# The second product of each filter tap contracts 128 rows instead of 64

## The chip, the cores and the metric

The kernel runs on one core of a Trainium2 chip. The metric is the time of one execution on the device in microseconds; a comparison uses the median of several runs. The engines of the core are named as in the profile: PE is TensorE (matrix products), PEld its weight loads, DVE is VectorE, ACT is ScalarE, POOL is GpSimd, and SP issues most of the DMA transfers.

## The reference, cut to what matters

The whole program is one layer: an input projection of 2048 tokens, a long convolution (branch A), a chunked gating unit (branch B) and an output projection. The change lies in the filter of the long convolution. Three sine layers give 64 features for each of 2048 positions, and one more product gives the taps of 1024 channels in both directions, which then decay with the position:

```python
def hyena_filter(L, w1, b1, fr1, w2, b2, fr2, w3, b3, fr3, w_o):
    ...
    h = jnp.sin(fr3.astype(f32) * (h @ w3.astype(f32) + b3.astype(f32)))
    h = h @ w_o.astype(f32)
    ...
    h_fwd = h[:, :D_A] * decay
    h_bwd = h[:, D_A:] * decay
    l1 = jnp.sum(jnp.abs(h_fwd), axis=0) + jnp.sum(jnp.abs(h_bwd[1:]), axis=0)
    k = jnp.concatenate([h_fwd, jnp.zeros((1, D_A), f32), h_bwd[1:][::-1]], axis=0)
    return k / (l1[None, :] + EPS)
```

## The kernel before

Tokens are kept as 16 groups j of 128. Every operand of a large product is split into a high part `hi` and a low part `lo` in the type float32r, and a product is three passes: hi by hi, lo by hi, hi by lo (`mm3`, L157 to L159).

The foreground is the input projection: 56 blocks of weights, each in four chunks of 512 tokens, each chunk 8 times `mm3` into one bank of PSUM. One chunk is a step. In the background run staged jobs, generators that are moved on by one stage at each step. The order in which the instructions of an engine stand is then settled by a scheduler that mixes foreground and background; on the chip each engine takes them in that fixed order.

The filter taps are the background of the first part (`k1_jobs`, with the foreground `ug_phase`). The channels go in two halves of 512. `k1_weights` loads the 64 rows of the filter's last weights twice, into rows 0 to 63 and again into rows 64 to 127 of `wr`, for each of the two directions d, and splits it into `hi` (ACT) and `lo` (DVE). Then 16 jobs `k1_job`, one for each j, two directions in each, so 2 x 16 x 2 = 64 taps products:

- `gd` (128 rows: the 64 features' high part in rows 0 to 63, their low part in rows 64 to 127) comes from DRAM by a DMA on POOL's queue (L444), in two buffers; `dd`, the decay, by a DMA on SP's queue (L446), also in two buffers.
- L452 multiplies all 128 rows of `gd` by all 128 rows of `wh`, which gives high by high and low by high in one product. L453 adds high by low: rows 0 to 63 of `gd` by rows 0 to 63 of `wl`. In the profile the rows of L452 read `a<-hi,gd` and those of L453 `a<-lo,gd`.
- DVE multiplies by the decay (L454), adds and subtracts the directions (L456, L457), ACT and DVE split the results (L150, L152), ACT takes the absolute value (L460) and DVE adds it to the running L1 sum (L461), which is the last reader of `dd`.
- A stage later the first step of a Fourier transform follows on PE: two `mm3` (rows `b<-hi,f` and `b<-lo,f`), copied out by ACT (L482) and written to DRAM (L483).

The job for j = 0 comes last in each half; it also takes the sum over all positions by two plain float32 products (L468).

Of the kernel before, what the change touches and what calls it, by code (L numbers as in the profile page):

```python
"""Hyena / gMLP hybrid block on one NeuronCore.  # L1

Tokens are kept in the order (j, p) with t = 16 p + j.  Every large product runs
as three float32r passes over operands split exactly into a high and a low part.
The long convolution is a 4096-point real DFT done as 256 x 16: one step over p,
one over j, a product of spectra, and the two steps back.
"""
# [5 lines left out]
F32 = mybir.dt.float32  # L13
# [17 lines left out]

# ---------------------------------------------------------------- constants
def _split(a):
# [76 lines left out]

# ------------------------------------------------------------------- kernel
class Body:
    """Foreground: the input projection, one chunk of 512 tokens a step.
    Background: staged jobs, each moved on by one stage a step."""

# [7 lines left out]

    # -- scheduling of the trace
    def go(self, job):
# [19 lines left out]

    # -- small helpers
    def split(self, eng, raw, pool, tag, bufs, copy=None):
        """Two float32r tiles whose sum is raw."""
        hi = pool.tile(list(raw.shape), F32R, name="hi", tag=tag, bufs=bufs)
        (copy or self.nc.scalar.copy)(hi, raw)  # L150
        lo = pool.tile(list(raw.shape), F32R, name="lo", tag=tag, bufs=bufs)
        eng.tensor_tensor(lo, raw, hi.bitcast(F32), op=ALU.subtract)  # L152
        return hi, lo
# [18 lines left out]

    # -- whole program
    def build(self):
# [82 lines left out]

    # -- x: RMS norm, transposed, split
    def x_phase(self, xs):
# [46 lines left out]

    # -- input projection
    def prep_w(self, blk, pool=None, tag="w", bufs=5, copy=None):
# [5 lines left out]
    def project(self, blk, nxt):  # L314
        """Yields (n, psum) of the block's four chunks of 512 tokens."""
        b, wh, wl = self.wq.pop(0)
        assert b == blk
        for n in range(4):
            if n == 1 and nxt is not None:
                self.prep_w(nxt)  # L320
            ps = self.bank("proj")
            for k in range(8):
                self.mm3(ps, wh[:, k], wl[:, k], self.xh[n][:, k], self.xl[n][:, k], k == 0, k == 7)
            yield n, ps

    # -- branch B: u * silu(gate)
    def ug_first(self, fg, xs):
# [5 lines left out]
    def silu(self, pool, ps, tag="sg", bufs=5):  # L333
        s = pool.tile([128, 512], F32, name="sg", tag=tag, bufs=bufs)
        self.nc.scalar.activation(s, ps, AF.Silu)
        return s
# [14 lines left out]

    # -- Hyena filter: features through the sine MLP
    def mlp(self, mp):
# [61 lines left out]

    # -- filter taps with decay, L1 norm, first DFT step
    def k1_jobs(self, kp):
# [10 lines left out]
    def k1_weights(self, kp, cs, st):  # L428
        nc, i = self.nc, self.i
        wo = i["filt_w_out"].rearrange("q (d c) -> q d c", d=2)[:, :, cs]  # L430
        st["w"] = []
        for d in range(2):
            wr = kp.tile([128, 512], F32, name="wr", tag="kq", bufs=10)
            for r in range(2):
                nc.sync.dma_start(wr[64 * r:64 * r + 64], wo[:, d])
            st["w"].append(self.split(nc.vector, wr, kp, "kw", 4))
        st["l1"] = kp.tile([128, 2, 512], F32, name="l1")
        nc.gpsimd.memset(st["l1"], 0.0)
        yield

    def k1_job(self, kp, cs, st, j):
        nc = self.nc
        gd = kp.tile([128, 2, 128], F32R, name="gd", bufs=2)
        nc.gpsimd.dma_start(gd, self.GD[j])  # L444
        dd = kp.tile([128, 2, 512], F32, name="dd", bufs=2)
        nc.sync.dma_start(dd, self.i["c_dec"][j][:, :, cs])  # L446
        yield
        l1 = st["l1"]
        for d in range(2):
            wh, wl = st["w"][d]  # L450
            ps = self.bank("a")
            nc.tensor.matmul(ps, gd[:, d], wh, start=True, stop=False)  # L452
            nc.tensor.matmul(ps, gd[0:64, d], wl[0:64], start=False, stop=True)  # L453
            nc.vector.tensor_tensor(dd[:, d], ps, dd[:, d], op=ALU.mult)  # L454
        s = [kp.tile([128, 512], F32, name="s", tag="kq", bufs=10) for _ in range(2)]
        nc.vector.tensor_tensor(s[0], dd[:, 0], dd[:, 1], op=ALU.add)  # L456
        nc.vector.tensor_tensor(s[1], dd[:, 0], dd[:, 1], op=ALU.subtract)  # L457
        if j:
            parts = [self.split(nc.vector, x, kp, "kq", 10) for x in s]
        nc.scalar.activation(dd, dd, AF.Abs)  # L460
        nc.vector.tensor_tensor(l1, l1, dd, op=ALU.add)  # L461
        if j == 0:
            sk = kp.tile([1, 512], F32, name="sk", tag="kq", bufs=10)
            nc.sync.dma_start(sk, self.i["hyena_skip"][cs].rearrange("(o c) -> o c", o=1))
            yield
            ps = self.bank("a")
            for d in range(2):
                nc.tensor.matmul(ps, self.ones, l1[:, d], start=d == 0, stop=d == 1)  # L468
            le, ri = l1[0:1, 0], l1[0:1, 1]
            nc.vector.tensor_scalar(le, ps[0:1], EPS, None, op0=ALU.add)  # L470
            nc.vector.tensor_tensor(sk, sk, le, op=ALU.mult)
            nc.vector.reciprocal(ri, le)
            nc.sync.dma_start(self.RB[cs].rearrange("(o c) -> o c", o=1), ri)
            for d in range(2):
                nc.vector.tensor_tensor(s[d][0:1], s[d][0:1], sk, op=ALU.add)
            parts = [self.split(nc.vector, x, kp, "kq", 10) for x in s]
        yield
        for d in range(2):
            ps = self.bank("b")
            self.mm3(ps, self.f1[:, 0, d], self.f1[:, 1, d], *parts[d])  # L480
            ev = kp.tile([128, 512], F32, name="ev", tag="kq", bufs=10)
            nc.scalar.copy(ev, ps)  # L482
            nc.sync.dma_start(self.AK[128 * d:128 * d + 128, j, cs], ev)  # L483

    # -- short convolution over a raw block with halo
    def halo(self, raw):
# [25 lines left out]
    def staggered(self, jobs):  # L512
        """One job a step."""
        for job in jobs:
            self.go(job)
            yield

    # -- branch A: u = conv(x1) conv(v), first DFT step
    def xv_phase(self):
# [37 lines left out]

    # -- branch A: conv(x0) * silu(gate) / l1
    def xg_phase(self):
# [18 lines left out]

    # -- branch B: layer norm, position mixing, gate
    def vb_phase(self):  # L580
# [33 lines left out]
    def gated(self, h, n, vr, ug):  # L614
        """Tokens 4 n .. of head h: the mixed values times u silu(gate)."""
        uv = ug.rearrange("d (j b p) -> d j b p", j=4, b=16)
        self.nc.vector.tensor_tensor(uv, uv, vr[:, :, 4 * n:4 * n + 4].rearrange("d b j p -> d j b p"), op=ALU.mult)
        self.nc.sync.dma_start(self.Y[4 * n:4 * n + 4, :, 8 + h].rearrange("j d p -> d j p"), ug.rearrange("d (j p) -> d j p", j=4))
# [40 lines left out]

    # -- second DFT step of both, product of spectra, first step back  # L660
    def fft_jobs(self, hf):
# [39 lines left out]

    # -- last DFT step, gate
    def inv_jobs(self):
# [30 lines left out]

    # -- output projection, post norm, residual
    def load_wo(self, n):
        """Rows 512 n .. of w_out, where chunk n of x was."""
        nc = self.nc
        hi = self.xp.tile([128, 4, D], F32R, name=f"woh{n}", tag=f"xh{n}")
        lo = self.xp.tile([128, 4, D], F32R, name=f"wol{n}", tag=f"xl{n}")  # L740
# [8 lines left out]
    def out_mms(self, ps, h, r, hi, lo):  # L749
        """Channel blocks 4 r .. of the products for half h of the outputs."""  # L750
        sl = slice(h * 512, h * 512 + 512)
        for q in range(4):
            self.mm3(ps, hi[:, q], lo[:, q], self.xh[r][:, q, sl], self.xl[r][:, q, sl], r == 0 and q == 0, r == 3 and q == 3)

    def first_tokens(self, j, rs):
        """Channel blocks 4 r .. of tokens j, split."""
        if j not in self.yq:
# [20 lines left out]
    def out_phase(self, op):  # L778
# [9 lines left out]
        ld = lambda: op.tile([128, 8, 128], F32, name="yraw", bufs=4)  # L788
        # What is wanted first lies where memory is free first.
        first = {"z": [z()], 0: [xt(0)], 3: [q(3)], 1: [xt(1)], 2: [q(2)], "ld": [ld()]}  # L790
# [74 lines left out]
```

## Time and profile before

| | |
|---|---|
| runs shown | 2061.54 us median of 3 (2061.28 to 2063.18) |
| span of the profiled execution, first to last instruction | 2056.8 us |
| median less span | 4.7 us |
| PE busy | 2011.0 us, 98% of the span |
| DVE, ACT, POOL busy | 1158.9, 765.2, 228.3 us |
| granted TensorE clock, mean | 0.997 |
| taps products on L452 and L453 | 64 each, between 139 and 449 us |

The page gives no time of its own for the profiled execution beside its span; the runs' times also hold what lies ahead of the first and behind the last instruction. Matrix products are pipelined, and a product's duration includes its way through the array, so what counts on PE is the distance from one start to the next.

### The profile page before, as it was taken

Reading aid. Unit: us, or ns where it says so; the run is one execution under the profiler, and the core shown is the slowest. Engines: PE = TensorE matmul, PEld = TensorE weight load, DVE = VectorE, ACT = ScalarE, POOL = GpSimd, SP = SyncE. Lnnn points to the kernel's source line nnn. Section 1 sums busy time; section 2 is a strip of 40 time slices with the busy share of each in tenths; the row PEclk is TensorE's granted clock in tenths of the full one; section 3 lists DMA queues with packets and bytes.
Section 4 is the critical chain, followed back from the end, with each engine's and each line's share of the span. In section 5 each row is a group of like instructions: output and inputs, shape, how many; then the busy total and the mean of one; then the engine's idle time right before and its main releaser. Section 6 shows DMA issues by size and latency. Waiting matters only on the chain. (4 is left out here: it accounts for less than half of the span.)

```text
span 2056.8 us, 24610 instructions
## 1 busy us (share of the span) xinstructions
PE 2011.0 (98%) x9000; PEld 1612.7 (78%) x9000; DVE 1158.9 (56%) x1906; ACT 765.2 (37%) x1333; POOL 228.3 (11%) x223
## 2 busy tenths in 40 slices
PE   6999999999999999999999999999999999999998
PEld 5776777778888877877777778878888887888887
DVE  7357555553333477788777766555666664322221
ACT  7134334333333455555444444343222243111111
POOL 1011011011000111111111111101101000101000
PEclk9999999999999999999999999999999999999999
DMA  6155434441222355445544544543546454522311
GB/s 212 48 146 193 145 118 148 144 141 57 62 62 62 108 154 152 144 145 171 160 150 149 152 156 154 164 149 118 164 144 202 149 169 165 185 83 92 113 62 41
DMA packets 189705, 274.22 MB, mean 133 GB/s; under 512 B 18027, under 2 KB 93803, under 8 KB 189551
## 3 DMA queue, kind: packets, MB, share of 16 engines
q1 hardware_dynamic: 175184, 250.56, 37.5%
q0 software_dynamic: 14112, 21.50, 4.3%
q8 instruction: 71, 1.16, 0.2%
q10 hardware_dynamic: 288, 0.59, 0.1%
q14 instruction: 50, 0.41, 0.1%
HBM read 179.26 MB, written 93.33 MB: 133 GB/s over the span
## 5 line engine op out<-in xcount | busy, mean ns | idle before, releaser
L157 PE MATMUL proj<-xh,hi 128*128 128x512 f32 x1792 | 710.4, 396 | 0.0
L158 PE MATMUL proj<-xh,lo 128*128 128x512 f32 x1792 | 703.0, 392 | 0.0
L159 PE MATMUL proj<-xl,hi 128*128 128x512 f32 x1792 | 702.5, 392 | 0.0
L157 PEld LDWEIGHTS proj<-xh,hi 128*128 128x128 f32 x1792 | 337.2, 188 | 74.1 <-issue 8.3
L159 PEld LDWEIGHTS proj<-xl,hi 128*128 128x128 f32 x1792 | 336.8, 188 | 70.4 <-issue 1.0
L158 PEld LDWEIGHTS proj<-xh,lo 128*128 128x128 f32 x1792 | 337.2, 188 | 68.9 <-issue 2.8
L152 POOL TENSOR_TENSOR lo<-wraw,hi 128x1024 fp32r<-128x1024 f32 x56 | 135.7, 2423 | 599.9 <-ACT hi L150 599.7
L158 PE MATMUL proj<-woh,q 128*128 128x512 f32 x448 | 174.4, 389 | 0.0
L159 PE MATMUL proj<-wol,q 128*128 128x512 f32 x448 | 174.3, 389 | 0.0
L157 PE MATMUL proj<-woh,q 128*128 128x512 f32 x448 | 174.1, 389 | 0.0
L152 DVE TENSOR_TENSOR lo<-raw,hi 128x512 fp32r<-128x512 f32 x192 | 133.3, 720 | 43.2 <-ACT hi L150 43.1
L499 DVE SCALAR_TENSOR_TENSOR t<-raw,cw,t 128x512 f32<-128x512 f32 x96 | 80.3, 840 | 108.1 <-ACT raw L490 54.4
L150 ACT CAST hi<-raw 128x512 fp32r<-128x512 f32 x192 | 112.1, 622 | 27.9 <-DMA raw<-BY 23.1
L507 ACT COPY raw<-proj 128x512 f32<-128x512 f32 x96 | 56.2, 587 | 166.4 <-PE proj L159 158.8
L150 ACT CAST hi<-pa 128x512 fp32r<-128x512 f32 x64 | 39.8, 622 | 200.0 <-DVE pa L693 187.3
L150 ACT CAST hi<-wraw 128x1024 fp32r<-128x1024 f32 x55 | 57.9, 1054 | 136.7 <-PE proj L158 84.1
L689 DVE TENSOR_TENSOR pa<-u,b 64x512 f32<-64x512 f32 x128 | 87.6, 684 | 37.0 <-PE b L159 18.7
L158 PEld LDWEIGHTS proj<-woh,q 128*128 128x128 f32 x448 | 84.1, 188 | 17.8 <-DVE q L801 0.3
L159 PEld LDWEIGHTS proj<-wol,q 128*128 128x128 f32 x448 | 84.1, 188 | 17.5
L157 PEld LDWEIGHTS proj<-woh,q 128*128 128x128 f32 x448 | 84.1, 188 | 17.3
L689 DVE TENSOR_TENSOR pb<-u,b 64x512 f32<-64x512 f32 x128 | 87.9, 686 | 1.9
L157 PE MATMUL b<-hi,tv 128*128 128x512 f32 x192 | 80.8, 421 | 8.0 <-ACT hi L150 6.4
(160 smaller groups left out, 2518.8 us busy)
## 6 DMA issues: line engine op xcount, KB each, us to landing
wraw<-in_w_in_dram SPq DMA_DIRECT2D x56, 512.0 KB, 3.7
xt<-in_x_dram SPq DMA_DIRECT2D x32, 512.0 KB, 4.9
dd<-in_c_dec_dram SPq DMA_DIRECT2D x32, 512.0 KB, 4.0
AK<-ev SPq DMA_DIRECT2D x64, 256.0 KB, 3.1
tv<-in_c_tv_dram POOLq DMA_DIRECT2D x64, 256.0 KB, 4.3
AU<-ev SPq DMA_DIRECT2D x64, 256.0 KB, 2.8
raw<-AU SPq DMA_DIRECT2D x64, 256.0 KB, 4.2
raw<-AK SPq DMA_DIRECT2D x64, 256.0 KB, 3.3
```

What stands on the lines that cost most here:

```text
L150: (copy or self.nc.scalar.copy)(hi, raw)
L152: eng.tensor_tensor(lo, raw, hi.bitcast(F32), op=ALU.subtract)
L157: t.matmul(ps, sh, mh, start=first, stop=False)
L158: t.matmul(ps, sl, mh, start=False, stop=False)
L159: t.matmul(ps, sh, ml, start=False, stop=last)
L499: nc.vector.scalar_tensor_tensor(v, raw[:, j0:j0 + 4], wv(0), v, op0=ALU.mult, op1=ALU.add)
L507: self.nc.scalar.copy(raw[:, 1 + 4 * n:5 + 4 * n].rearrange("q j p -> q (j p)"), ps)
L689: nc.vector.tensor_tensor(o, uu, kk, op=ALU.mult)
```

## The change

The low part of the weights, `lo`, gets zeros in rows 64 to 127 (a MEMSET on POOL of 64 x 512 for each of the two directions in each of the two halves, four in all, L437 of the changed kernel), and the second product takes all 128 rows of both operands. The added rows multiply the low part of the features by zero, so the sum stays what it was. Nothing else is edited but comments; behind the edit the lines of the changed kernel are two higher (L452 becomes L454, L453 becomes L455).

```diff
@@ k1_weights
             for r in range(2):
                 nc.sync.dma_start(wr[64 * r:64 * r + 64], wo[:, d])
-            st["w"].append(self.split(nc.vector, wr, kp, "kw", 4))
+            hi, lo = self.split(nc.vector, wr, kp, "kw", 4)
+            nc.gpsimd.memset(lo[64:128].bitcast(F32), 0.0)
+            st["w"].append((hi, lo))
@@ k1_job
             nc.tensor.matmul(ps, gd[:, d], wh, start=True, stop=False)
-            nc.tensor.matmul(ps, gd[0:64, d], wl[0:64], start=False, stop=True)
+            nc.tensor.matmul(ps, gd[:, d], wl, start=False, stop=True)
```

The scheduler orders a stretch of PE's program and a few rows of POOL's anew. DVE and SP keep their order, ACT's differs by one copy that moves ahead by a place.

On PE, at the first taps products of the program, there stood before (proj rows are the foreground's products, `a` the bank of the taps):

```order
L158 MATMUL proj<-xh_87,lo 128x512
L452 MATMUL a<-hi,gd 128x512
L159 MATMUL proj<-xl_88,hi 128x512
L157 MATMUL proj<-xh_87,hi 128x512
L453 MATMUL a<-lo,gd 128x512
L158 MATMUL proj<-xh_87,lo 128x512
L159 MATMUL proj<-xl_88,hi 128x512
L157 MATMUL proj<-xh_87,hi 128x512
L452 MATMUL a<-hi,gd 128x512
L158 MATMUL proj<-xh_87,lo 128x512
L159 MATMUL proj<-xl_88,hi 128x512
L453 MATMUL a<-lo,gd 128x512
```

and now stands there:

```order
L158 MATMUL proj<-xh_87,lo 128x512
L454 MATMUL a<-hi,gd 128x512
L159 MATMUL proj<-xl_88,hi 128x512
L157 MATMUL proj<-xh_87,hi 128x512
L158 MATMUL proj<-xh_87,lo 128x512
L159 MATMUL proj<-xl_88,hi 128x512
L157 MATMUL proj<-xh_87,hi 128x512
L455 MATMUL a<-lo,gd 128x512
L454 MATMUL a<-hi,gd 128x512
L158 MATMUL proj<-xh_87,lo 128x512
L159 MATMUL proj<-xl_88,hi 128x512
L157 MATMUL proj<-xh_87,hi 128x512
```

The first two second products stand three foreground products later than before. Some thirty places on, at the Fourier products of the fifth job, PE had before:

```order
L157 MATMUL proj<-xh_85,hi 128x512
L158 MATMUL proj<-xh_85,lo 128x512
L159 MATMUL proj<-xl_86,hi 128x512
L157 MATMUL b<-hi,f_205 128x512
L158 MATMUL b<-hi,f_205 128x512
L157 MATMUL proj<-xh_85,hi 128x512
```

and has now:

```order
L157 MATMUL proj<-xh_85,hi 128x512
L158 MATMUL proj<-xh_85,lo 128x512
L159 MATMUL proj<-xl_86,hi 128x512
L157 MATMUL proj<-xh_85,hi 128x512
L157 MATMUL b<-hi,f_205 128x512
L158 MATMUL b<-hi,f_205 128x512
```

One foreground product moved ahead of the Fourier products. Behind the tenth second product no second product moves against its neighbours, and behind this stretch PE's order is the old one to the end. On POOL, where the taps begin, the rows before were:

```order
L152 TENSOR_TENSOR lo<-wraw,hi 128x1024 x6
L438 MEMSET l_943 128x1024
L444 DMA gd<-GD 128x256 x7
L152 TENSOR_TENSOR lo<-wraw,hi 128x1024
L444 DMA gd<-GD 128x256 x3
```

and are now:

```order
L152 TENSOR_TENSOR lo<-wraw,hi 128x1024 x6
L440 MEMSET l_945 128x1024
L446 DMA gd<-GD 128x256 x2
L437 MEMSET lo 64x512 x2
L446 DMA gd<-GD 128x256 x5
L152 TENSOR_TENSOR lo<-wraw,hi 128x1024
L446 DMA gd<-GD 128x256 x3
```

The two MEMSETs stand behind the loads of the first two jobs and ahead of the third's. The other two, for the second half of the channels, stand just ahead of the second MEMSET of `l`.

## Rows read from the trace of the kernel before

**Rows 1.** The page, part 1: busy us (share) xinstructions of each engine.

```profile
PE 2011.0 (98%) x9000; PEld 1612.7 (78%) x9000; DVE 1158.9 (56%) x1906; ACT 765.2 (37%) x1333; POOL 228.3 (11%) x223
```

**Rows 2.** Windows by stage: length, busy time by engine, granted clock, DMA share, GB/s.

```profile
139.00:172.00 33.00, 31.29 (x116) 20.89 (x117) 25.25 (x35) 17.19 (x27) 5.59 (x6) 1.00 0.60 189
172.00:450.00 278.00, 278.00 (x1128) 208.71 (x1127) 155.84 (x211) 103.99 (x158) 35.80 (x37) 1.00 0.45 150
450.00:2057.00 1607.00, 1580.37 (x7193) 1284.67 (x7191) 902.54 (x1538) 588.28 (x1042) 168.79 (x165) 1.00 0.41 130
```

**Rows 3.** Timeline from 302 us, PE and PEld: start, duration, engine, line, tiles [wait].

```profile
302.53 0.39 PE L157 MATMUL proj<-xh,hi 128*128 128x512 f32 x1
...
303.66 0.39 PE L159 MATMUL proj<-xl,hi 128*128 128x512 f32 x1
303.67 0.19 PEld L452 LDWEIGHTS a<-hi,gd 128*128 128x128 f32 x1
303.89 0.39 PE L452 MATMUL a<-hi,gd 128*128 128x512 f32 x1
...
304.21 0.18 PEld L453 LDWEIGHTS a<-lo,gd 64*128 64x128 f32 x1 [0.35 <-issue]
304.21 0.50 PE L453 MATMUL a<-lo,gd 64*128 64x512 f32 x1
...
304.64 0.49 PE L452 MATMUL a<-hi,gd 128*128 128x512 f32 x1
...
305.06 0.50 PE L453 MATMUL a<-lo,gd 64*128 64x512 f32 x1
...
305.49 0.50 PE L157 MATMUL proj<-xh,hi 128*128 128x512 f32 x1
...
305.82 0.39 PE L158 MATMUL proj<-xh,lo 128*128 128x512 f32 x1
...
312.40 0.39 PE L452 MATMUL a<-hi,gd 128*128 128x512 f32 x1
```

**Rows 4.** Windows of line L453 alone: length, PE busy, PEld busy, clock, DMA.

```profile
172.00:450.00 278.00, 26.89 (x54) 9.87 (x54) 1.00 0.45 150
139.00:172.00 33.00, 4.97 (x10) 1.83 (x10) 1.00 0.60 189
```

**Rows 5.** Timeline from 154 to 172 us, the first jobs, all engines.

```profile
154.38 0.55 SPq L446 DMA_DIRECT2D dd<-in_c_dec_dram  x1
...
159.02 0.69 DVE L454 TENSOR_TENSOR dd<-a,dd 128x512 f32<-128x512 f32 x1 [0.66 <-DMA dd<-in_c_dec_dram]
159.62 1.22 DVE L461 TENSOR_TENSOR l<-l,dd 128x1024 f32<-128x1024 f32 x1
...
165.53 0.69 DVE L454 TENSOR_TENSOR dd<-a,dd 128x512 f32<-128x512 f32 x1 [1.19 <-DMA dd<-in_c_dec_dram]
...
167.27 2.94 POOL L152 TENSOR_TENSOR lo<-wraw,hi 128x1024 fp32r<-128x1024 f32 x1 [2.86 <-ACT hi L150]
...
168.01 0.50 PE L159 MATMUL b<-lo,f 128*128 128x512 f32 x1 [0.16 <-DVE lo L152]
...
168.66 2.10 DVE L456 TENSOR_TENSOR s<-dd 128x512 f32<-128x512 f32 x1
...
170.79 0.62 ACT L150 CAST hi<-s 128x512 fp32r<-128x512 f32 x1 [1.66 <-DVE s L456]
...
171.47 0.50 PE L157 MATMUL b<-hi,f 128*128 128x512 f32 x1 [1.34 <-ACT hi L150]
```

**Rows 6.** Timeline at 140 us and at 281 us: second products, and the splits ahead of them.

```profile
140.40 0.69 DVE L152 TENSOR_TENSOR lo<-wr,hi 128x512 fp32r<-128x512 f32 x1 [1.33 <-ACT hi L150]
...
142.07 0.50 PE L453 MATMUL a<-lo,gd 64*128 64x512 f32 x1
...
281.37 0.67 DVE L152 TENSOR_TENSOR lo<-wr,hi 128x512 fp32r<-128x512 f32 x1
```

**Rows 7.** Groups of POOL's instructions: busy us, mean ns of one, idle before.

```profile
L438 POOL MEMSET l<- 128x1024 f32 x2 | 1.9, 957 | 13.0 <-DVE s L475 13.0
```

## The prediction

> **What bounds the kernel now.** I read the page first. PE is busy for 2011.0 of 2056.8 us [rows 1], but pipelined products overlap, so that share only says where to look. The windows by stage show how tight PE is. From 172 to 450 us, where most of the taps are computed, it is busy for the whole 278.00 us, at a granted clock of 1.00 (the full 2.4 GHz); from 139 to 172 us it lacks 1.71 us of 33.00; behind 450 us it lacks 26.6 us of 1607.00 [rows 2]. DVE is busy for 155.84 of the 278.00 us, ACT and POOL for less. So in the long middle stretch PE waits for nobody, and what shortens its stream there shortens the program. Nothing behind 450 us hangs on a fixed moment: its waits are on chains that start from PE's own earlier products, and the whole stretch moves ahead with them.
>
> Next I read the timeline of PE and its weight loads around two taps products in that stretch, by distances from start to start [rows 3]. The foreground's products follow each other every 0.227 us (302.53 to 303.89 is six steps, 1.36 us). The first product L452 keeps that step (303.66 to 303.89, 0.23 us), and its weight load starts at 303.67, a whole step ahead of its product. At L453 the rhythm breaks. Its weight load starts at 304.21, in the same moment as its product, after 0.35 us in which the load path stood idle for no releaser. The steps from 303.89 on are 0.32, 0.43, 0.42, 0.43 and 0.33 us; the first foreground product behind the pair has a duration of 0.50 in place of 0.39 us, so it is not the second product alone that pays. Five steps take 1.93 us, where five of 0.227 would take 1.13. That is 0.80 us too many for two second products: **0.40 us for each**.
>
> The reader should see what does not explain it. L452 and L453 read the same `gd`, write the same bank and follow each other without a semaphore; L452 has the rhythm and L453 has not. What differs is that L453 takes 64 rows (`64*128` and `64x512`) and everything around it takes 128. PE pays once going in and once coming out.
>
> A rule speaks against the change: the Trainium skill, "TensorE: Matmul & The Clock Gate", section "Why this matters for your kernels", says that a product with a short contraction takes as long as one with 128 rows, and "LDWEIGHTS (loading the stationary operand)" that a load's time goes by columns. The loads agree with it, 0.18 against 0.19 us [rows 3]; by this rule alone nothing would be gained, 2061.5 us, and that is the first rival below. Against it stands "TensorEngine Tiling (Array Packing)", section "Key Properties": changing the tiling mode drains the array. By that the excess goes away with the 64 rows, and the stretched steps of the trace are on its side.
>
> **What the change removes.** 64 second products of 64 rows; ten of them lie before 172 us and 54 behind [rows 4]. The trace has no `a<-lo,gd` of 128 rows. Its step is bounded by 0.227 us (L452, the same form with the same stationary operand) from below and by 0.43 us (as today) from above [rows 3]; I take the lower one, since every 128-row product beside it has it. For the 54, which lie where PE has no wait, the sum is 54 x 0.40 = 21.6 us.
>
> **The ten in the start.** The ten would give 4.0 us, but I expect them to be lost. Up to 171 us five jobs run densely, and what sets their pace is a loop through the decay tile `dd`, which has two buffers: DVE's L461 of a job is the last reader, SP then issues the next load (154.38), DVE's L454 takes it up at 159.02 after a wait for that DMA, L461 of that job stands behind it (159.62 plus 1.22 us), and the next L454 starts at 165.53, again after a wait for the DMA [rows 5]. The loop goes round in 6.5 us without PE. DVE's order is unchanged, so PE cannot pull it. PE in fact waits for it already: 0.16 us at 168.01, and 1.34 us at 171.47 for ACT's `hi` of the fifth job [rows 5]. What PE gains in the ten it will stand and wait there. All that remains is the order: one foreground product now stands ahead of that wait and not behind it, which is worth one step, 0.2 us.
>
> **A port in the start.** The wait at 171.47 is as late as it is because L456 took 2.10 us where another DVE operation of that shape takes 0.69 [rows 5, 6]; POOL's L152 on the next weights ran beside it, from 167.27 for 2.94 us, and L456 ends, at 170.76, half a microsecond behind POOL: roughly its own length after POOL let go. ACT's `hi` at 170.79 and PE's product at 171.47 follow from that. POOL's L152 comes, through ACT, from a foreground product, so it will start earlier by what PE gained so far, up to 1 us, and may meet other DVE work. Freed of POOL the chain would be 1.4 us earlier (2.10 less 0.69); if POOL comes ahead of L461 or the split behind it, the chain is later by up to one more hold, 2.94 less the 1.4 already paid, 1.5 us. I take a loss of 0.3 us and keep -1.4 and +1.5 for the range.
>
> **What the change adds.** Four MEMSETs of 64 x 512 on POOL. One of 128 x 1024 takes 0.96 us [rows 7], and half its length bounds mine between nothing and 0.96; by elements in a row I estimate 0.5 us. Their own time lies beside PE's work. What could cost is the wait: the second product now waits for the MEMSET, which waits for DVE's split. For the second direction, the tighter one, the split ends at 140.40 + 0.69 = 141.09, the MEMSET by my estimate at about 141.7. L453 there started at 142.07 [rows 6]; it now stands three foreground products later (0.68 us), behind a stream that is shorter by 0.40 us for the first second product and 0.1 us for its own entry, so at about 142.25. It is covered with half a microsecond to spare, and just covered if the MEMSET takes 0.96. What stands behind the MEMSETs on POOL's queue is the load of `gd` for the third job, which had to wait anyway for L453 of the first, just past 142.57. In the second half the last split starts at 281.37 [rows 6], and the first second product is at 304.21 [rows 3], so this pair costs PE nothing; if it held DVE through the port as above, the Fourier products of the last job of the first half could be late by up to one MEMSET, 0.96 us, which the range holds.
>
> **Sum.** 21.6 + 0.2 - 0.3 = 21.5 us. The profiled span is 2056.8 us, from which 2035.3 follows; the runs hold 4.7 us more than the span, which the change does not touch. From the median of 2061.5 the forecast is **2040.0 us**.
>
> **Rivals.**
> 1. *The excess is not the row count's.* If it belonged to the second product as the one that closes the bank's sum, or if a 128-row load here still could not start ahead, steps stay 0.42 and the time stays 2061.5. For it: no 128-row second product is in the trace. Against it: the foreground's products, which close banks too, all keep the plain step [rows 3]. The same skill page, "Part 3: Packing small matmuls", says that a load overlaps a running product only where the row groups differ, which full rows do not; the loads at 303.67 and before run beside products of 128 rows all the same, so the trace does not bear it out. Chance 0.04.
> 2. *The start is not lost.* If DVE's loop is pulled by PE after all, all 64 count: 64 x 0.40 = 25.6 us, 2035.9. For it: ACT, which stands between DVE's halves of a job, also copies PE's results out, so an earlier PE frees it earlier. Against it: the loop's waits for its own DMA, above. Chance 0.12.
> 3. *Part is given back.* If the denser stream brings PE up to a chain of DVE in the middle stretch, some 5 to 15 us of the 21.5 return as waits: 2045 to 2055. Against it: DVE has 44% of that stretch free, and a job's round of 8.5 us there (303.89 to the next job's L452 at 312.40) [rows 3] is well above the loop's 6.5 even when it is 0.8 shorter. Chance 0.08.
> 4. *Slower.* If the MEMSET held POOL's queue or PE for more than 10.8 us in each of its two places (half of 21.5), the waits outweigh the gain; at twice that, 21.6 us each, the time is 2083. The nearest price is 0.96 us, more than ten times below the point where it decides. Chance 0.02.
>
> The forecast's own chance is 0.74. Its range is 2038 to 2042; 8 in 10 with the rivals next to it (all 64 saved, the first part of the give-back) is 2035 to 2044. What a measurement of this kernel can tell from no change is 0.2%, 4 us. So faster 0.94, same 0.04, slower 0.02.
>
> **What the profile after should show.** Right: second products as `128*128`, each 0.23 us behind its predecessor, loads a step ahead; a job's round in the middle stretch 7.7 in place of 8.5 us; the PE wait for ACT's `hi` of the fifth job grown by about 4 us and still ending near 171 us, the end of the taps about 21 us earlier, and the same distance from there to the end. Wrong: steps of 0.43 that stay (rival 1), a start that ends near 167 us (rival 2), PE waits on DVE between 172 and 430 us (rival 3), or PE's waits naming the MEMSET (rival 4).

## The result and the profile after

The changed kernel takes 2043.25 us (median of 5 runs, 2038.34 to 2044.73) beside 2061.39 us of the kernel before (5 runs, 2060.93 to 2063.18): a ratio of 0.9906, 95% interval 0.9893 to 0.9919. It is faster by 18.1 us. A second set of runs gave 2041.85 us beside 2059.67, a ratio of 0.9914 (0.9901 to 0.9928). The forecast was 2040.0 us: the measured time lies outside its range of 2038 to 2042 and inside the wider one of 2035 to 2044, and the gain is 3.4 us short of the 21.5 forecast.

The second products first. From the timeline of the changed kernel, PE and one weight load, around one taps job of the middle stretch; these rows answer to [rows 3]:

```profile
306.07 0.39 PE L454 MATMUL a<-hi,gd 128*128 128x512 f32 x1
306.07 0.19 PEld L455 LDWEIGHTS a<-lo,gd 128*128 128x128 f32 x1
306.30 0.39 PE L455 MATMUL a<-lo,gd 128*128 128x512 f32 x1
306.52 0.39 PE L454 MATMUL a<-hi,gd 128*128 128x512 f32 x1
306.75 0.39 PE L455 MATMUL a<-lo,gd 128*128 128x512 f32 x1
306.98 0.39 PE L157 MATMUL proj<-xh,hi 128*128 128x512 f32 x1
307.20 0.39 PE L158 MATMUL proj<-xh,lo 128*128 128x512 f32 x1
```

The five steps from 306.07 on take 1.13 us, where they took 1.93 before [rows 3]. The rhythm runs through the pair unbroken, the weight load of L455 starts at 306.07, a whole step ahead of its product, and the foreground product behind the pair is back at 0.39 us. The windows by stage of the same kernel, with the columns of [rows 2]:

```profile
139.00:172.00 33.00, 27.83 (x110) 20.31 (x111) 25.95 (x34) 16.76 (x27) 6.95 (x8) 0.96 0.59 185
172.00:430.00 258.00, 258.00 (x1126) 212.21 (x1126) 152.24 (x208) 104.02 (x157) 35.21 (x37) 0.99 0.50 160
430.00:2042.00 1612.00, 1583.27 (x7201) 1287.34 (x7199) 907.28 (x1542) 587.98 (x1043) 169.72 (x168) 1.00 0.42 130
```

In the middle stretch PE still has no gap, and it runs 1126 products in 258 us where 1128 took 278 [rows 2]. In the start it is worse than before: 27.83 busy us of 33.00 where there were 31.29, and a granted clock of 0.96.

Three lengths, taken from the starts of products in each timeline, say where the time went. The start reaches from the first L452 (in the changed kernel L454) to the eleventh, the first of the sixth job; the middle from there to the last second product; the rest from there to the end of the span.

| profile | start | middle | rest | span |
|---|---|---|---|---|
| before | 36.54 | 272.80 | 1608.25 | 2056.8 |
| before, second profile | 37.88 | 272.78 | 1611.70 | 2060.9 |
| changed | 39.70 | 251.62 | 1611.65 | 2042.2 |
| changed, second profile | 39.65 | 251.62 | 1611.17 | 2040.7 |

The middle gave 21.2 us. The start took 3.2 back. The rest is 3.4 us longer than in the first profile of before, and no longer than in the second.

What happened in the start is in the timeline of the changed kernel, DVE, POOL and PE, from 158 us; the rows answer to [rows 5]:

```profile
158.90 0.69 DVE L456 TENSOR_TENSOR dd<-a,dd 128x512 f32<-128x512 f32 x1 [1.48 <-DMA dd<-in_c_dec_dram]
...
165.63 0.69 DVE L456 TENSOR_TENSOR dd<-a,dd 128x512 f32<-128x512 f32 x1 [1.53 <-DMA dd<-in_c_dec_dram]
166.24 1.22 DVE L463 TENSOR_TENSOR l<-l,dd 128x1024 f32<-128x1024 f32 x1
...
166.39 3.26 POOL L152 TENSOR_TENSOR lo<-wraw,hi 128x1024 fp32r<-128x1024 f32 x1 [2.75 <-ACT hi L150]
...
167.37 2.83 DVE L152 TENSOR_TENSOR lo<-s,hi 128x512 fp32r<-128x512 f32 x1
...
170.25 0.79 PE L159 MATMUL b<-lo,f 128*128 128x512 f32 x1 [3.30 <-DVE lo L152]
...
170.85 0.63 PE L159 MATMUL proj<-xl,hi 128*128 128x512 f32 x1
...
171.27 0.63 PE L157 MATMUL proj<-xh,hi 128*128 128x512 f32 x1
...
174.26 0.63 PE L157 MATMUL b<-hi,f 128*128 128x512 f32 x1
```

DVE takes up a decay tile every 6.7 us (158.90 to 165.63), each time after a wait of about 1.5 us for its DMA; those waits were 0.66 and 1.19 before [rows 5]. POOL's split of a block of weights now begins at 166.39, while DVE's L463 runs. The next DVE operation, the split of the taps, takes 2.83 us in place of 0.69 [rows 6], and PE waits 3.30 us for it. Then PE's step is 0.43 us, not 0.23 (170.85 to 171.27), and durations are 0.63. The windows around it show why (last columns: granted clock, DMA share, GB/s):

```profile
165.00:170.00 5.00, 1.96 (x9) 1.29 (x7) 4.37 (x3) 2.02 (x3) 3.26 (x1) 0.92 0.45 132
170.00:172.00 2.00, 1.75 (x4) 1.46 (x5) 1.90 (x4) 0.92 (x2) 0.00 (x0) 0.50 0.85 283
172.00:177.00 5.00, 5.00 (x15) 3.86 (x15) 2.72 (x4) 2.39 (x4) 0.00 (x0) 0.60 0.66 215
177.00:180.00 3.00, 3.00 (x15) 2.47 (x14) 0.82 (x2) 0.59 (x1) 0.00 (x0) 1.00 0.53 190
```

At the end of PE's wait and behind it the granted clock is 0.50 (1.2 GHz), and it is back at 1.00 by 177 us; from the means of these windows the stretch reaches from about 169.2 to 176.0 us. That lower clock is in none of the prediction's terms.

### The profile page after: what moved, and what is told of

Same layout as the page of the kernel before. It is cut to its first block, busy times and chain, and to the rows that moved or that the text cites. A ratio compares the mean times of both kernels' runs of the same rounds, so it can differ in the third digit from the quotient of the medians.

```text
span 2042.2 us, 24620 instructions
## 1 busy us (share of the span) xinstructions
PE 1991.0 (97%) x9000; PEld 1618.6 (79%) x9000; DVE 1160.2 (57%) x1906; ACT 764.4 (37%) x1333; POOL 230.0 (11%) x227
## 5 line engine op out<-in xcount | busy, mean ns | idle before, releaser
L152 POOL TENSOR_TENSOR lo<-wraw,hi 128x1024 fp32r<-128x1024 f32 x56 | 135.7, 2422 | 602.2 <-ACT hi L150 602.0
L152 DVE TENSOR_TENSOR lo<-raw,hi 128x512 fp32r<-128x512 f32 x192 | 133.4, 720 | 45.5 <-ACT hi L150 45.1
L150 ACT CAST hi<-pa 128x512 fp32r<-128x512 f32 x64 | 39.7, 620 | 199.6 <-DVE pa L695 186.9
```

## The experiments

Lengths are named as in the table above. Single runs stand beside a run of the kernel before at 2063.89 us on the same chip; runs of one kernel scatter by some us (the kernel before from 2055.4 to 2064.6 over 17 runs), so there the steps and the lengths decide, not the time.

**One direction at 128 rows.** Only the second product of direction 1 takes all rows.

```diff
-            nc.tensor.matmul(ps, gd[:, d], wl, start=False, stop=True)
+            rows = slice(0, 128 if d else 64)
+            nc.tensor.matmul(ps, gd[rows, d], wl[rows], start=False, stop=True)
```

> The second product of direction 0 keeps 64 rows, that of direction 1 takes 128. Theory A (each 64-row product among 128-row ones costs 0.40 us, none for 128 rows): steps around direction 0 stay 0.32 and 0.43 us with 0.33 behind, direction 1 runs at 0.23; behind the start the 27 products of direction 1 save 27 x 0.40 = 10.8 us, so the time lies about 10.8 us above the changed kernel's middle stretch, near 2050. Rival (the gain is not the row count's): no change of steps, or all steps shortened alike.

Measured: 2048.48 us, middle 262.31, which is 10.5 us below before; 10.8 were expected. The timeline shows both kinds side by side:

```profile
300.61 0.39 PE L454 MATMUL a<-hi,gd 128*128 128x512 f32 x1
300.93 0.50 PE L456 MATMUL a<-lo,gd 64*128 64x512 f32 x1
301.36 0.50 PE L454 MATMUL a<-hi,gd 128*128 128x512 f32 x1
301.69 0.39 PE L456 MATMUL a<-lo,gd 128*128 128x512 f32 x1
301.92 0.39 PE L157 MATMUL proj<-xh,hi 128*128 128x512 f32 x1
```

The 64-row product is stretched going in (0.32) and out (0.43 and 0.33), the 128-row product of the same job leaves at 0.23. The cost belongs to the form, as theory A has it. The start is 37.87 us long. It has a PE wait of 3.31 us at 170.75, as long as the one in the changed kernel, but here the granted clock stays at 1.00 from 165 to 180 us.

**Two 64-row products side by side.** The kernel before, with both first products of a job ahead of both second ones. They stand side by side in 26 of the 27 jobs of the middle; in the start, and in the last job, the scheduler puts other products between them.

```diff
+        pss = [self.bank("a") for _ in range(2)]
         for d in range(2):
-            wh, wl = st["w"][d]
-            ps = self.bank("a")
-            nc.tensor.matmul(ps, gd[:, d], wh, start=True, stop=False)
-            nc.tensor.matmul(ps, gd[0:64, d], wl[0:64], start=False, stop=True)
-            nc.vector.tensor_tensor(dd[:, d], ps, dd[:, d], op=ALU.mult)
+            nc.tensor.matmul(pss[d], gd[:, d], st["w"][d][0], start=True, stop=False)
+        for d in range(2):
+            nc.tensor.matmul(pss[d], gd[0:64, d], st["w"][d][1][0:64], start=False, stop=True)
+        for d in range(2):
+            nc.vector.tensor_tensor(dd[:, d], pss[d], dd[:, d], op=ALU.mult)
```

> The kernel before with the two 64-row products of a job side by side, behind both 128-row products. Theory A1 (PE pays where the row count changes): steps into the pair 0.32, inside the pair about 0.23, out 0.43 and 0.33 us, an excess of 0.40 us a job in place of 0.80, so 27 x 0.40 = 10.8 us less behind the start, near 2050. Rival A2 (every 64-row product pays by itself, whatever stands beside it): the step inside the pair is 0.43 too, the excess 0.60 to 0.80 us a job, the time between 2056 and 2061.

Measured: 2048.64 us, middle 263.07, 9.7 us below before; 10.8 were expected. From the timeline, PE and the weight loads of the pair:

```profile
308.53 0.39 PE L451 MATMUL a<-hi,gd 128*128 128x512 f32 x1
308.85 0.18 PEld L453 LDWEIGHTS a<-lo,gd 64*128 64x128 f32 x1 [0.35 <-issue]
308.85 0.49 PE L453 MATMUL a<-lo,gd 64*128 64x512 f32 x1
308.95 0.19 PEld L453 LDWEIGHTS a<-lo,gd 64*128 64x128 f32 x1
309.18 0.39 PE L453 MATMUL a<-lo,gd 64*128 64x512 f32 x1
309.50 0.50 PE L157 MATMUL proj<-xh,hi 128*128 128x512 f32 x1
309.84 0.40 PE L158 MATMUL proj<-xh,lo 128*128 128x512 f32 x1
```

The steps from 308.53 on are 0.32, 0.33, 0.32 and 0.34 us. The step inside the pair is not the 0.23 that I expected, and the way out is 0.32, not 0.43. The sum is as expected all the same: four steps take 1.31 us where four of 0.227 would take 0.91, an excess of 0.40 us a job in place of 0.80. The same split fits the kernel before: a change of the row count stretches the step into it by about 0.09 us and the step behind it by about 0.11, and where a 64-row product stands alone the second share of one change and the first of the next fall into one step, 0.43 us [rows 3]. So PE pays about 0.20 us for each change of the row count, and not for each product of 64 rows: half the changes, half the cost, and rival A2 is out. No run has three 64-row products in a row, so that one away from any change keeps 0.23 us is not shown. The Trainium skill, "TensorEngine Tiling (Array Packing)", section "Key Properties", says that a change of the tiling mode drains the array. The trace agrees in so far as the cost lies at the change; what the array does there, no run shows.

**32 rows.** The contribution of rows 32 to 63 of the low part is left out.

```diff
-            nc.tensor.matmul(ps, gd[0:64, d], wl[0:64], start=False, stop=True)
+            nc.tensor.matmul(ps, gd[0:32, d], wl[0:32], start=False, stop=True)
```

> The kernel before with a second product of 32 rows; the contribution of rows 32 to 63 of the low part is left out. Theory A1 (a change of row count costs, not the number of rows): the same steps of 0.32, 0.43 and 0.33 us, 0.40 us for each product, the time of the kernel before, 2061 us. Rival (the cost grows with the rows that are missing): an excess of 0.6 us or more for each, 2071 us or more.

Measured: 2057.7 us, inside the scatter of the kernel before, and a middle of 273.49 beside 272.80. The timeline has the steps 0.32, 0.42, 0.43, 0.42 and 0.34:

```profile
303.42 0.39 PE L452 MATMUL a<-hi,gd 128*128 128x512 f32 x1
303.74 0.50 PE L453 MATMUL a<-lo,gd 32*128 32x512 f32 x1
304.16 0.50 PE L452 MATMUL a<-hi,gd 128*128 128x512 f32 x1
304.59 0.49 PE L453 MATMUL a<-lo,gd 32*128 32x512 f32 x1
305.01 0.50 PE L157 MATMUL proj<-xh,hi 128*128 128x512 f32 x1
305.35 0.39 PE L158 MATMUL proj<-xh,lo 128*128 128x512 f32 x1
```

How many rows are missing makes next to no difference (0.7 us over 54 products); the rival is out.

**The MEMSETs alone.** The kernel before with the four MEMSETs, the product still at 64 rows.

```diff
-            st["w"].append(self.split(nc.vector, wr, kp, "kw", 4))
+            hi, lo = self.split(nc.vector, wr, kp, "kw", 4)
+            nc.gpsimd.memset(lo[64:128].bitcast(F32), 0.0)
+            st["w"].append((hi, lo))
```

> The kernel before with the four MEMSETs added and the second product still at 64 rows. Theory (they are covered): steps and PE waits as before, 2061 us within 2 us. Rival (the MEMSET and its wait cost): PE waits that name it at 140 or 276 us, up to 1 us each.

Measured: 2063.14 us, middle 272.81, and no PE wait names the MEMSET. The start is 37.63 us with a PE wait of 2.78 for DVE's split at 169.70, which the kernel before has as well in its second profile (below). The MEMSETs cost nothing that shows.

**Three buffers for the decay tile**, on the changed kernel.

```diff
-        dd = kp.tile([128, 2, 512], F32, name="dd", bufs=2)
+        dd = kp.tile([128, 2, 512], F32, name="dd", bufs=3)
```

> The changed kernel with three buffers for the decay tile in place of two. Theory B (the start is paced by the loop through the two buffers): DVE's waits for the decay's DMA between 150 and 170 us go, the five jobs come every 5.5 us or so in place of 6.6, PE's wait of 3.3 us at 170 us shrinks to under 2 us, and 4 to 7 us come off: 2036 to 2039. Rival (the start is paced by DVE itself or by POOL holding it): PE's wait stays above 3 us, the time within 2 us of the changed kernel's 2043.

Measured: 2035.67 us (4 runs, 2033.61 to 2038.33), ratio to before 0.9884 (0.9870 to 0.9898), 6.2 us below the changed kernel on the same chip. The start is 32.88 us. In its timeline DVE takes up a new decay tile without a wait:

```profile
154.20 0.68 DVE L456 TENSOR_TENSOR dd<-a,dd 128x512 f32<-128x512 f32 x1
...
159.74 0.68 DVE L456 TENSOR_TENSOR dd<-a,dd 128x512 f32<-128x512 f32 x1
...
163.01 2.64 POOL L152 TENSOR_TENSOR lo<-wraw,hi 128x1024 fp32r<-128x1024 f32 x1 [5.44 <-DMA AK<-ev]
163.29 2.90 DVE L459 TENSOR_TENSOR s<-dd 128x512 f32<-128x512 f32 x1
...
166.85 0.50 PE L159 MATMUL b<-lo,f 128*128 128x512 f32 x1 [0.99 <-DVE lo L152]
```

A job comes every 5.54 us (154.20 to 159.74), where the loop took 6.7 in the changed kernel and 6.5 in the kernel before [rows 5]. POOL still holds DVE (L459 takes 2.90 us), but DVE is now early enough that PE waits 0.99 us for it, and the granted clock stays at 1.00 from 165 to 180 us. Theory B holds for the changed kernel, with one reserve: given the third buffer, the scheduler also orders DVE's and PE's programs anew in the start, and no run has the one without the other.

**One block's split moved from POOL to DVE**, on the changed kernel; it is the split that begins at 166.39.

```diff
-        self.wq.append((blk,) + self.split(self.nc.gpsimd, raw, pool, tag, bufs, copy))
+        eng = self.nc.vector if blk == 51 else self.nc.gpsimd
+        self.wq.append((blk,) + self.split(eng, raw, pool, tag, bufs, copy))
```

> The changed kernel with the split of one block of weights, the one that POOL did at 166 us, done by DVE. Theory C (POOL's split holds DVE's split of the taps from 167.4 to 170.2 us, and the long PE wait lets the clock fall): that split takes 0.69 in place of 2.83 us, PE's wait at 170 us falls to some 1 us with another of about 1 us behind it, the clock stays at 1.00 between 165 and 180 us, 3 to 4 us come off: 2039 to 2040. Rival (DVE would be late anyway): the wait stays 3 us and the time 2043.

Measured: 2038.97 us (5 runs, 2036.45 to 2043.96), ratio 0.9904 (0.9887 to 0.9921), 2.9 us below the changed kernel. The start is 34.78 us, 4.9 below it. From the timeline of DVE:

```profile
166.68 0.68 DVE L152 TENSOR_TENSOR lo<-s,hi 128x512 fp32r<-128x512 f32 x1
167.29 0.68 DVE L457 TENSOR_TENSOR dd<-a,dd 128x512 f32<-128x512 f32 x1
167.89 1.22 DVE L152 TENSOR_TENSOR lo<-wraw,hi 128x1024 fp32r<-128x1024 f32 x1
```

The split of the taps is back at 0.68 us, PE's wait is 1.18 us, and the clock between 165 and 180 us is 1.00. Theory C holds for the start; the interval of the time overlaps that of the changed kernel, so the 2.9 us are not settled by the time alone. The second wait of about 1 us that I expected behind it did not come.

**Both edits together.**

```diff
-        self.wq.append((blk,) + self.split(self.nc.gpsimd, raw, pool, tag, bufs, copy))
+        eng = self.nc.vector if blk == 51 else self.nc.gpsimd
+        self.wq.append((blk,) + self.split(eng, raw, pool, tag, bufs, copy))
...
-        dd = kp.tile([128, 2, 512], F32, name="dd", bufs=2)
+        dd = kp.tile([128, 2, 512], F32, name="dd", bufs=3)
```

> Both edits of the two experiments ahead. Theories B and C together: nothing of PE's gain in the start is lost, PE runs from 140 us on with waits of under 1 us in sum, all 64 products count: 25.6 us below the kernel before, 2035 to 2037. Rival (each edit alone already removes the one wait there is): no faster than the better of the two.

Measured: 2036.11 us (4 runs, 2032.48 to 2038.07), ratio 0.9884 (0.9869 to 0.9899), start 32.37. That is in the expected range, but 23.6 us below the kernel before on the same chip and not the 25.6 expected, with PE waits of 0.96 and 0.45 us in the start where under 1 us in sum was expected. It is no faster than the third buffer alone: with the buffer the start has only some 1 us of PE's wait for DVE left to save. The rival is right on this point, and the third buffer alone is the version to keep.

**The changed kernel again.** No edit.

> The changed kernel unedited, beside its variants on the same chip: 2043 us, with runs from 2038 to 2045; the runs with the lower time have the higher mean clock.

Measured: 2041.85 us (4 runs, 2040.77 to 2043.47). The start is 39.65 us, with the same PE wait (3.46 us at 170.30) and a granted clock of 0.89 from 165 to 180 us where the first profile has 0.77. The clocks of its four runs (0.997 and 0.998) are too close together to say whether they order the times. In the five runs of the result they do: 2038.34 us at a mean clock of 1.000, then 0.998, 0.996, 0.995 and 2044.73 us at 0.995.

**Three buffers on the kernel before.** The edit of `dd` above, with the 64 rows kept.

> The kernel before, 64 rows kept, with three buffers for the decay tile. Theory B (the loop through the decay tile bounds the start only where PE would be faster than it): PE's own stream needs 6.0 us a job there and loses 1.5 to 2.8 us by waits, so at most 1 to 3 us come off, 2057 to 2059 beside 2060. Rival (the third buffer is worth its 6 us whatever the products cost): 2054.

Measured: 2059.67 us (12 runs, 2055.22 to 2062.71) beside 2060.25, ratio 0.9998 (0.9987 to 1.0008). The start is 35.59 us, 1.0 to 2.3 below the two profiles of before, and the time does not show it: 0.6 us where 1 to 3 were expected, with an interval from 2.7 us faster to 1.6 slower. The rival, 6 us, is out. The buffer is worth its 6 us only behind the change. With the 64-row products PE's own stream in the start comes to 34.1 us (132 steps and 4.2 us of excess, below), 6.8 a job in the mean, which is no shorter than the loop; without their excess it is 6.0, and the loop sets the pace. The expectation put 6.0 where 6.8 belongs.

**The kernel before again.** No edit.

> The kernel before unedited, a second profile. The time less the span is 1.8 us as in the other runs. If POOL's split meets DVE in the start by a margin of under half a microsecond, either L456 takes 2.1 us and PE waits 1.3 us (as in the first profile), or DVE's split takes 2.8 us and PE waits 2.8; the stretch behind the taps, 1608 us in the first profile, comes out between 1607 and 1613.

Measured: 2062.68 us, 1.8 us above the span. Its timeline in the start, and below it the same place in the first profile:

```profile
166.09 1.22 DVE L461 TENSOR_TENSOR l<-l,dd 128x1024 f32<-128x1024 f32 x1
166.93 2.59 POOL L152 TENSOR_TENSOR lo<-wraw,hi 128x1024 fp32r<-128x1024 f32 x1 [2.86 <-ACT hi L150]
167.23 2.83 DVE L152 TENSOR_TENSOR lo<-s,hi 128x512 fp32r<-128x512 f32 x1
...
170.12 0.50 PE L159 MATMUL b<-lo,f 128*128 128x512 f32 x1 [2.60 <-DVE lo L152]
```

```profile
166.14 1.22 DVE L461 TENSOR_TENSOR l<-l,dd 128x1024 f32<-128x1024 f32 x1
167.27 0.69 DVE L152 TENSOR_TENSOR lo<-s,hi 128x512 fp32r<-128x512 f32 x1
167.88 0.68 DVE L454 TENSOR_TENSOR dd<-a,dd 128x512 f32<-128x512 f32 x1
```

In the first profile POOL came at the end of L461 (at 167.27, [rows 5]) and DVE's split took its 0.69 us; here POOL comes 0.34 us earlier, DVE's split is held for 2.83 us, and PE waits 2.60. The kernel before stands on an edge here and falls to either side: the kernel with 32 rows to that of the first profile (PE waits 1.36 us for ACT's `hi`), the ones with the MEMSETs alone and with the pair side by side to the other (2.78 and 2.76 us for DVE's `lo`). The rest is 1611.70 us, 3.4 above the first profile. Over all the profiles of this document it lies between 1607.5 and 1612.6 us, and both ends are kernels without the change (32 rows, and the MEMSETs alone); so the 3.4 us of the changed kernel lie within the scatter and are not shown to be the change's.

## Why the prediction was right, and where its sum was off

**The excess and its cause** were right. PE pays 0.40 us for each 64-row product between 128-row ones, in the start as in the middle, and nothing for 128 rows; the middle gave 21.2 us of the 21.6 forecast. A job's round there is 7.71 us (298.36 to 306.07), as forecast. That it is the change of the row count, and not the last product of a sum or a 128-row load that cannot start ahead (rival 1), is shown by the steps of the changed kernel, by the pair side by side and by the 32 rows.

**The start** was right in its mechanism and mis-sized. Its 132 steps of 0.227 us make 29.9 us. In the first profile of before, 1.8 us of excess stand at PE's waits and 4.2 in the 30 steps into, out of and behind the ten 64-row products, and 0.6 are small stretches elsewhere: 36.5. In the changed kernel the waits make 5.7 us, the steps at the lower clock 2.8, and 1.3 are left: 39.7. So the waits grew by 3.9 us where the ten products gave 4.2, and they were lost as the prediction said. That the decay tile's two buffers pace the start is seen in DVE's longer waits for the tile, and the third buffer bears it out. One reading of that loop was wrong: the L461 at 159.62 us is not that of the job whose L454 starts at 159.02, but of the job ahead, whose L456, L457 and ACT's absolute value come before it; it stands behind that L454 in DVE's order, and the round of 6.5 us remains. What the prediction left out is the 2.8 us of the granted clock at 0.50 around the end of the long wait (1.7 us in the second profile, where the waits make 6.9 and the start is as long). The term "0.2 less 0.3" should have read -3.2 against the first profile of before, or -1.8 against the second.

**The hold by POOL** had been priced from -1.4 to +1.5 us, with POOL ahead of DVE's split as the late case. That case came, and the price was too low. The wait moved from ACT's `hi` of the fifth job, where I looked for it, one place ahead to DVE's `lo` of the fourth, and grew to 3.30 us; the Fourier product of the fifth job came at 174.26 in place of 171.47, 2.8 us later. The moved split shows the cause: without the hold the start is 4.9 us shorter, of which 2.8 are the lower clock; by these numbers that clock is what carried the case past +1.5. The page "SBUF — State Buffer" of the Trainium skill, section "SBUF: two separate sides", describes such a hold: the pair of ports is locked for a whole instruction by a GpSimd operation or by a DVE operation with two inputs in SBUF, whichever starts first, where the GpSimd operation reads SBUF. The rows agree: the held ones (DVE's L152 here, L456 in the first profile of before, L459 in the kernel with three buffers) have both inputs in SBUF, while L454 at 167.88 us of the first profile of before, which has one input in PSUM, took its 0.68 us in the middle of POOL's operation.

**The MEMSETs** were covered, as forecast; their time on the chip was estimated at 0.5 us, and the group of them in the changed kernel's profile reads (shortest, median and longest in ns)

```profile
L437 POOL MEMSET lo<- x4: 521/522/523, 139.9 to 276.6; 64x512 f32 x4
```

**The time around the span** was wrong: not 4.7 but 1.8 us, in every run whose span is known. So the profiled execution of before, whose own time is not on record, ran at about 2058.6 us by this estimate, 2.8 below the median; the forecast came out at 2040.0 because it took the gain from the median, which this does not touch.

**The sum.** By the profiles: middle -21.2, start +3.2, rest +3.4, together -14.6 us of span. By the medians it is -18.1. The difference lies in which execution of before was profiled: against its second profile the changed kernel's span is shorter by 18.7 us: 21.2 from the middle, less 1.8 in the start and 0.7 ahead of the first taps product (139.28 beside 138.55 us). The end of the taps came 17.9 us earlier than in the first profile (430.60 beside 448.53 us), not the 21 forecast.

**Rival 2** (all 64 count) did not come about. The third buffer comes near it: 2035.67 us beside 2059.67 of the kernel before on the same chip is 24.0 us, of the 25.6 that all 64 would give. **Rival 3** is out: PE is busy for all of the 258 us from 172 to 430. **Rival 4** is out with the MEMSETs alone.

## What to carry to other kernels

A product with fewer rows that stands alone between full ones breaks PE's rhythm twice, 0.40 us in this kernel, and zeros in the spare rows mend that; its sign in a trace is a weight load that begins together with its product, with no releaser named. A gain on PE ends where the next loop takes over, here a tile with two buffers filled by DMA, so a third buffer whose worth no time showed before the change was worth 6.2 us behind it.

## What the runs showed of the hardware

A PE wait of 3.30 us came with a granted clock of 0.50 until about 176 us in the first profile of the changed kernel; a wait of 3.31 us in the same place in the kernel with one direction changed did not, with a clock of 1.00 from 165 to 180 us. Near 1107 us, waits of 2.07 and 2.09 us stand in the two profiles of the changed kernel: behind the first the clock is 0.50 from 1107.9 to 1111.2 us, behind the second it is 1.00. So the same wait may or may not cost clock. In the five runs of the result the time goes with the mean clock (2038.34 us at 1.000, 2044.73 at 0.995), and such stretches are likely part of their scatter of 6 us; what else is in it, and in the 9 us of the kernel before, stays open.

Each change between 128 and 64 rows costs PE about 0.20 us at the full clock, about 0.09 in the step into it and 0.11 in the step behind it, for 32 rows as for 64. Right at a change the weight load begins together with its product (308.85 us, and [rows 3]); the load of the next product, here one of 64 rows too, starts 0.23 us ahead of it again (308.95).
